# Binding the decay differences in VectorE's order, and taking the first token tile's low inputs last in the mixer's output product

## The chip, the cores and the metric

The kernel runs on one core of one Trainium2 chip. The metric is the device time of one execution in microseconds (us), median over several runs. The engines are named as in the profile: PE is TensorE (PEld its weight loads), DVE is VectorE, ACT is ScalarE, POOL is GpSimd, SP is the engine whose queue issues most DMAs.

## What is computed

A decoder trunk of two layers over 256 tokens of width 1024, all in float32. Each layer is a half-step SwiGLU feed-forward, a token mixer with two branches side by side, and a second feed-forward:

```python
for l in range(DEPTH):
    h = h + 0.5 * swiglu(rms_norm(h, ffn1_norm[l]), ffn1_w_in[l], ffn1_w_out[l])
    u = rms_norm(h, mix_norm[l])
    (z_s, xbc, dt_s, qkv, z_d, b_d, a_d, gate_s, gate_d) = split(u @ w_in[l])
    y_s = mamba2_branch(z_s, xbc, dt_s, ...)     # SSD scan, 32 heads in 4 groups, chunks of 128
    y_d = deltanet_branch(qkv, z_d, b_d, a_d, ...)  # gated delta rule, 8 heads, chunks of 64
    merged = (sigmoid(gate_s) * (y_s @ ssm_w_branch[l])
              + sigmoid(gate_d) * (y_d @ dn_w_branch[l]))
    h = h + merged @ w_out[l]
    h = h + 0.5 * swiglu(rms_norm(h, ffn2_norm[l]), ffn2_w_in[l], ffn2_w_out[l])
return rms_norm(h, final_norm)
```

Inside the SSD scan each group of 8 heads needs a decay matrix per chunk: the exponential of the differences of a cumulative sum, with a causal mask, times the product of C and B.

```python
seg = a_cum[:, :, :, None] - a_cum[:, :, None, :]
decay = where(causal, exp(where(causal, seg, 0.0)), 0.0)
cb = einsum("bclgn,bcsgn->bclsg", Cc, Bc)
y_diag = einsum("bclsg,bclsgh,bcsghp->bclghp", cb, decay, xdt)
```

## The kernel before

Weights come from memory as tiles of 128 x 1024 float32 (`wraw`). Every float32 product is made of three products of rounded parts: each weight tile is split into a high part (`whi`, a copy on ScalarE) and a low part (`wlo`, a subtraction on VectorE), each input in the same way (`mh` and `ml` in the mixer's output product, `bh` and `bl` in the branches), and TensorE adds high x high, high x low and low x high (`mm3`). Five raw tiles and five split pairs are in flight; the splits are made ahead of the products that use them.

The kernel is written with a tile framework. It sorts each engine's instructions into one fixed queue before the run: it walks them in the order of the program with estimates of its own for their durations, and gives an idle engine the earliest instruction of the program that is ready. So an instruction that stands late in the program can be put early into a queue, wherever the estimate sees a hole. `tc.issue_after(ins)` adds an edge without a semaphore: what is traced inside it comes behind `ins` in the queue of the same engine. On the chip each queue is run in its order.

The mixer follows a list of steps, `ORDER`. The end of it is

```python
R x00 R d1 x01 R d3 R R P R g100 g101 D0 S0 x10 T0 D1
x11 g110 g111 S1 x20 T1 o x21 N D2 y S2 D3 x30 x31 T2 g000 g010 g001 S3 g011 T3
```

`R` is a step of DeltaNet's recurrence over chunks (`recur`); its last steps write the sum `vb` on VectorE from the PSUM bank `ob`. `P` (`ssd_pre`) multiplies B and C for the four groups (`cbb` on TensorE, four PSUM banks in rotation with other tiles named by `trb`) and masks them on VectorE (`cbm`, which is `cbt` in the profile). `Dg` (`decay`) makes group g's decay matrix `dc`, 128 x 2048: a broadcast DMA from `rdram` on SP's queue, then the difference to `ac` (VectorE), a minimum with 0 (VectorE), the exponential (ScalarE) and the product with `cbm` (VectorE). `xgi` projects two of a group's channels and convolves them (`ca` on ScalarE and VectorE, then `xsT` on ScalarE). `Sg` and `Tg` are the two halves of the scan of a group: transposes of `xsT` into `xsb` and the scaled inputs `xD`, `xdt`, `xe`; then the products with `dc` into `ydb`. `zgi` and `gsni` are projections that give gates. `o` and `N` are DeltaNet's branch: `dn_T` turns and splits a pair of heads of `vb` (`oT`, `og`, `bh`, `bl`), and `dn_branch` multiplies with the branch weights (`b`). `y` is `ss_T(0)`, the same for the first piece of the SSD output `yz` (`yT`); the SSD branch itself follows the list. Then `merge` adds the two branches into `tg`, turns them (`mT`) and splits them into `mh` and `ml`, one token tile t of 128 tokens after the other, and `close` runs the output product (`o` in the profile, lines 335 to 337 for high x high, high x low, low x high) through `out_chunks`: first the weight tiles 0 and 1 as one group, both halves n of the output columns, for t = 0 and then for t = 1.

Of the kernel before, what the change touches and what calls it, by code (L numbers as in the profile page):

```python
# [11 lines left out]
ALU = mybir.AluOpType  # L12
# [4 lines left out]
P = 128  # L17
D = 1024
S = 256
# [34 lines left out]
def trunk_kernel(ctx, tc, x, wst, wsm, norms, lpar, rpar, cst, out):  # L54
    nc = tc.nc
    V, A, G, PE = nc.vector, nc.scalar, nc.gpsimd, nc.tensor
# [10 lines left out]
    def act(o, i, func=AF.Copy, **kw):  # L67
        return A.activation(out=o, in_=i, func=func, **kw)  # L68

    def tt(o, a, b, op):  # L70
        return V.tensor_tensor(out=o, in0=a, in1=b, op=op)  # L71
# [4 lines left out]
    def ts(o, a, s1, op0, sc2=None, op1=None):  # L76
        if op1 is None:
            return V.tensor_scalar(out=o, in0=a, scalar1=s1, scalar2=None, op0=op0)
        return V.tensor_scalar(out=o, in0=a, scalar1=s1, scalar2=sc2, op0=op0, op1=op1)

    def f(ap):
        return ap.bitcast(F32)
# [66 lines left out]
    state = {"loaded": 0, "prepped": 0, "taken": 0, "last": None, "hold": False, "behind": {}, "late": {}, "first": 0, "turns": {}, "first_chunk": False, "cap": n_forms}  # L149
# [69 lines left out]
    h = cpool.tile([P, 2, D], F32, name="h")  # L219
# [11 lines left out]
    ident = cs[:, 0:P]  # L231
# [102 lines left out]
    def mm3(ps, lh, ll, rh, rl, start, stop):  # L334
        PE.matmul(ps, lh, rh, start=start, stop=False)  # L335
        PE.matmul(ps, lh, rl, start=False, stop=False)  # L336
        return PE.matmul(ps, ll, rh, start=False, stop=stop)  # L337
# [55 lines left out]
                        cut and a == 0 and kt == 1,  # L393
                    )

    def out_chunks(ps, stat, ks, last, group=1, split=False, first=None):

        for g0 in range(0, len(ks), group):
            kk = ks[g0 : g0 + group]
            ws = [(k, take()) for k in kk]  # L400
            for t in range(2):
                order = [(k, n) for n in range(2) for k in range(len(kk))]
                if t == 1 and not split:
                    m = len(kk) - 2 if len(kk) == NSPL else len(kk)
                    order = [(k, n) for k in range(m) for n in range(2)]
                    order += [(k, n) for n in range(2) for k in range(m, len(kk))]
                order = [(k, n, 0, 512) for k, n in order]
                if t == 1 and split:
                    order = [o for o in order if o[1] == 0]
                    order += [(k, 1, c, c + 256) for c in (0, 256) for k in range(len(kk))]  # L410
                state["sums"] = []
                for k, n, c0, c1 in order:
                    k, (wh, wl) = ws[k]
                    sh, sl = stat(k, t)
                    c = slice(n * 512 + c0, n * 512 + c1)
                    begin = k == 0 if first is None else first and t == n == 1
                    bank = ps[t][n][:, c0:c1]
                    if c0:
                        begin, bank = k == kk[0], ps[2][:, 0:256]
                    ins = mm3(bank, sh, sl, wh[:, c], wl[:, c], begin, k == last)  # L420
                    state["sums"].append(ins)

    def residual(po, nw):
        def add(t):
# [11 lines left out]

    def close(po, stat, n_k, nw):

        out_chunks(po, stat, list(range(2)), n_k - 1, group=2)
        out_chunks(po, stat, list(range(2, n_k - NSPL)), n_k - 1)  # L440
        state["hold"] = True
        out_chunks(po, stat, list(range(n_k - NSPL, n_k)), n_k - 1, group=NSPL, split=nw is None)
        return residual(po, nw)
# [149 lines left out]
    def mixer(l, nxt):  # L593
# [13 lines left out]
        yz = {}  # L607
# [37 lines left out]
        ac = small([P, 2, 40], "ac", 1)  # L645
# [380 lines left out]
        late = {}  # L1026
# [11 lines left out]
        def ssd_pre():  # L1038
            BT, CT = late["BC"][:, 0:4], late["BC"][:, 4:8]
            cbt = slots.tile([P, 3 * GS, P], F32, tag="sF", name="cbt")  # L1040
            late["cbx"] = cbx = cbt[:, 2 * GS :]
            late["cbm"] = cbm = cbt[:, : 2 * GS].rearrange("p (g t) l -> p g t l", g=GS)
            for g in range(GS):
                cbb = trb("cbb")
                PE.matmul(cbb[:, 0 : 2 * P], BT[:, g, 0:P], CT[:, g, :], start=True, stop=True)
                PE.matmul(cbb[:, 2 * P : 3 * P], BT[:, g, P : 2 * P], CT[:, g, P : 2 * P], start=True, stop=True)
                tt(
                    cbm[:, g],
                    cbb[:].rearrange("p (t o l) -> p t o l", t=2, o=2)[:, :, 0, :],
                    U[:, None, :].to_broadcast([P, 2, P]),  # L1050
                    ALU.mult,
                )
                act(cbx[:, g], cbb[:, P : 2 * P])
            yield

        xsT = {}
# [2 lines left out]
        def decay(g):  # L1059
            dc = slots.tile([P, 8, 2, P], F32, tag=("sA", "sB")[g % 2], name="dc")  # L1060
            nc.sync.dma_start(
                dc[:].rearrange("p h t l -> p (h t l)"),
                rdram[8 * g : 8 * g + 8].rearrange("a b -> (a b)").partition_broadcast(P),
            )
            tt(
                dc[:], dc[:],
                ac[:, :, 8 * g : 8 * g + 8].rearrange("p t h -> p h t")[:, :, :, None].to_broadcast([P, 8, 2, P]),
                ALU.subtract,
            )
            dv = dc[:].rearrange("p h t l -> p (h t l)")  # L1070
            ts(dv, dv, 0.0, ALU.min)
            act(dv, dv, AF.Exp)
            tt(dc[:], dc[:], late["cbm"][:, g, None].to_broadcast([P, 8, 2, P]), ALU.mult)
            decs[g] = dc

        def xs_unit(g, i):
# [73 lines left out]
        def dn_T(hp):  # L1150
            bank = trb("oT")
            bv = bank[:].rearrange("p (a c i) -> p a c i", a=2, c=4)
            for c in range(4):
                PE.transpose(bv[:, :, c, :], vb[:, c, hp, :], ident)
            og = tmp2("og")
            stt(og[:], bank[:], dnw, late["zdT"][:, 2 * hp : 2 * hp + 2, :].rearrange("p h t -> p (h t)"), ALU.mult, ALU.mult)
            oh = s2.tile([P, 2, S], F32R, tag="s2", name="bh")
            ol = s2.tile([P, 2, S], F32R, tag="s2", name="bl")
            act(oh[:].rearrange("p a t -> p (a t)"), og[:])
            tt(ol[:].rearrange("p a t -> p (a t)"), og[:], f(oh[:]).rearrange("p a t -> p (a t)"), ALU.subtract)  # L1160
            brT[("d", hp)] = (oh, ol)

        def ss_T(j):
            bank = trb("yT")
            g, k0 = j // 2, (j % 2) * 2
            for k in range(2):
                for t in range(2):
                    c0 = (k0 + k) * P
                    PE.transpose(bank[:, k * S + t * P : k * S + (t + 1) * P], yz[g][:, t, c0 : c0 + P], ident)
            oh = s2.tile([P, 2, S], F32R, tag="s2", name="bh")  # L1170
            ol = s2.tile([P, 2, S], F32R, tag="s2", name="bl")
            for k in range(2):
                w = snw[:, 2 * j + k : 2 * j + k + 1]
                act(oh[:, k], bank[:, k * S : (k + 1) * S], scale=w)
                stt(ol[:, k], bank[:, k * S : (k + 1) * S], w, f(oh[:, k]), ALU.mult, ALU.subtract)
            brT[("s", j)] = (oh, ol)

        def branch(kind, n, mk, tail=1):
            ps = [[accb("b"), accb("b")] for _ in range(2)]
            held = {}  # L1180

            def stat(k, t):
                oh, ol = held[k // 2]
                return oh[:, k % 2, t * P : (t + 1) * P], ol[:, k % 2, t * P : (t + 1) * P]

            made = 1
            for j0 in list(range(n - tail)) + [n - tail]:
                js = range(j0, j0 + (tail if j0 == n - tail else 1))
                while made < min(js[-1] + 2, n):
                    mk(made)  # L1190
                    made += 1
                for j in js:
                    held[j] = brT.pop((kind, j))
                out_chunks(ps, stat, [2 * j + i for j in js for i in range(2)], 2 * n - 1, group=2 * len(js))
            return ps

        def dn_branch():
            ps = branch("d", 4, dn_T)
            m = tg[1]
            for t in range(2):  # L1200
                for n in range(2):
                    sl = slice(n * 512, (n + 1) * 512)
                    stt(m[:, t, sl], m[:, t, sl], 1.0, ps[t][n][:], ALU.add, ALU.mult)
# [49 lines left out]
        ps = branch("s", 8, ss_T)  # L1253
# [185 lines left out]
```

## Time and profile before

| | |
|---|---|
| median of 3 runs | 1543.27 us (1543.04 to 1545.02) |
| the profiled execution | 1541.48 us |
| its span, first to last instruction | 1539.7 us |
| busy: PE, DVE, ACT, POOL | 1522.8, 1229.7, 944.8, 81.8 us |
| mean granted TensorE clock | 0.999 |

The profile comes from one execution. A timeline row gives the start from the span's beginning, the duration, the engine, the line of the kernel, the operation, the tiles written and read, the shapes and a count; in brackets the idle time of the engine before it and what ended it. Many elementwise operations go through helpers, so their line is the helper's (68 for ScalarE, 71, 74 and 78 for VectorE) and the tiles' names tell them apart. A matmul's duration holds its way through the array; successive matmuls overlap, so distances between starts tell what one takes in a row of them. Both layers' mixers run the same queues; the first stands at about 190 to 600 us of the span, the second some 760 us later.

### The profile page before, as it was taken

The page shows a single profiled execution, that of the slowest core. Times are in us where ns is not written, and L with a number is a line of the kernel's source. Part 1 is how long each engine was busy: PE and PEld are TensorE (multiplying, and loading weights), DVE is VectorE, ACT ScalarE, POOL GpSimd, SP SyncE. Part 2 cuts the span into 40 slices and gives each one's busy share as a digit, 9 for nine tenths or more (in the row PEclk, how much of TensorE's full clock was granted, in tenths as well). Part 3 has the DMA queues.
Part 4 walks back from the last instruction along what each step waited for, and adds up shares of the span by engine and source line. Part 5 has one row for each costly group of instructions (what it writes and reads, how often), then busy time and mean ns, then how long its engine had stood idle before and what let it go on. Part 6 is the DMA issues. An engine that isn't in the chain of part 4 may idle for free.

```text
span 1539.7 us, 29072 instructions
## 1 busy us (share of the span) xinstructions
PE 1522.8 (99%) x11473; PEld 1384.4 (90%) x11473; DVE 1229.7 (80%) x1859; ACT 944.8 (61%) x1532; POOL 81.8 (5%) x92
## 2 busy tenths in 40 slices
PE   8999999999999999999999999999999999999998
PEld 7999889999888888999899998899998888899997
DVE  6878769967899766789778887689589996677886
ACT  5655667765665645555555566676756666455565
POOL 0000110000000000000100012010000000000010
PEclk9999999999999999999999999999999999999999
DMA  7687775653565556587867687665345555556785
GB/s 277 190 265 231 226 228 167 187 164 111 178 213 171 163 166 196 185 256 211 261 225 225 208 253 229 197 193 180 117 141 202 179 170 186 176 177 195 247 241 156
DMA packets 98831, 305.73 MB, mean 199 GB/s; under 512 B 22837, under 2 KB 23813, under 8 KB 97670
## 3 DMA queue, kind: packets, MB, share of 16 engines
q1 hardware_dynamic: 93796, 290.95, 57.2%
q0 software_dynamic: 4608, 12.58, 5.1%
q8 instruction: 90, 1.47, 0.4%
q14 instruction: 47, 0.39, 0.1%
q10 hardware_dynamic: 290, 0.33, 0.1%
HBM read 297.72 MB, written 1.92 MB: 195 GB/s over the span
## 4 chain that ended last, share of the span: by engine, by line
PE 89%; DVE 4%; ACT 2%; DMA 2%; issue 1%; SPq 1%; POOL 0%; POOLq 0%; ACTq 0%; DVEq 0%
PE fc L346 10%; PE fc L340 9%; PE fc L345 9%; PE t L366 9%; PE o L337 4%; PE o L335 4%; PE o L336 4%; PE f L366 3%; PE b L335 3%; PE b L337 3%; PE b L336 3%; PE p L336 2%; PE p L337 2%; PE p L335 2%; PE xs L345 1%; PE xs L340 1%
## 5 line engine op out<-in xcount | busy, mean ns | idle before, releaser
L71 DVE TENSOR_TENSOR wlo<-wraw,whi 128x1024 fp32r<-128x1024 f32 x488 | 591.8, 1221 | 186.7 <-ACT whi L68 172.2
L68 ACT ACTIVATE whi<-wraw 128x1024 fp32r<-128x1024 f32 x488 | 511.6, 1059 | 271.0 <-PE fc L345 92.5
L346 PE MATMUL fc<-uW,wlo 128*128 128x256 f32 x1280 | 354.9, 277 | 0.0
L340 PE MATMUL fc<-uW,whi 128*128 128x256 f32 x1280 | 354.1, 277 | 0.0
L345 PE MATMUL fc<-uW,whi 128*128 128x256 f32 x1260 | 348.3, 276 | 0.0
L340 PEld LDWEIGHTS fc<-uW,whi 128*128 128x128 f32 x1280 | 240.5, 188 | 0.8
L346 PEld LDWEIGHTS fc<-uW,wlo 128*128 128x128 f32 x1280 | 240.5, 188 | 0.0
L345 PEld LDWEIGHTS fc<-uW,whi 128*128 128x128 f32 x1260 | 236.5, 188 | 0.8
L366 PE MATMUL t<-whi,uW 128*128 128x512 f32 x512 | 165.3, 397 | 0.0
L366 PEld LDWEIGHTS t<-whi,uW 128*128 128x128 f32 x512 | 95.9, 188 | 21.6 <-issue 1.3
L68 ACT ACTIVATE whi<-wsum 128x1024 fp32r<-128x1024 f32 x64 | 68.0, 1062 | 58.8 <-PE fc L345 32.9
L366 PE MATMUL t<-wlo,uW 128*128 128x512 f32 x256 | 100.2, 392 | 0.0
L71 DVE TENSOR_TENSOR wlo<-wsum,whi 128x1024 fp32r<-128x1024 f32 x64 | 78.2, 1221 | 7.9 <-ACT whi L68 5.6
L335 PE MATMUL b<-whi,bh 128*128 128x512 f32 x192 | 76.1, 398 | 0.3
L336 PE MATMUL b<-wlo,bh 128*128 128x512 f32 x192 | 74.9, 390 | 0.0
L337 PE MATMUL b<-whi,bl 128*128 128x512 f32 x192 | 74.2, 393 | 0.0
L340 PE MATMUL xs<-uW,whi 128*128 128x256 f32 x256 | 72.8, 284 | 0.0
L346 PE MATMUL xs<-uW,wlo 128*128 128x256 f32 x256 | 71.4, 279 | 0.0
L345 PE MATMUL xs<-uW,whi 128*128 128x256 f32 x254 | 70.6, 278 | 0.0
L335 PE MATMUL o<-whi,gh 128*128 128x512 f32 (+1 forms) x160 | 62.0, 388 | 0.0
L337 PE MATMUL o<-whi,gl 128*128 128x512 f32 (+1 forms) x160 | 61.8, 386 | 0.0
L336 PE MATMUL o<-wlo,gh 128*128 128x512 f32 (+1 forms) x160 | 61.7, 386 | 0.0
(337 smaller groups left out, 3291.7 us busy)
## 6 DMA issues: line engine op xcount, KB each, us to landing
wraw<-in_wst_dram SPq DMA_DIRECT2D x504, 512.0 KB, 4.9
wsum<-in_wst_dram SPq DMA_DIRECT2D x16, 512.0 KB, 7.3
wsum<-in_wst_dram POOLq DMA_DIRECT2D x16, 512.0 KB, 8.7
dc<-rdram SPq DMA_DIRECT2D x8, 1024.0 KB, 8.5
nw<-in_norms_dram SPq DMA_DIRECT2D x6, 512.0 KB, 5.9
h<-u POOLq DMA_DIRECT2D x12, 256.0 KB, 6.8
gb<-rdram SPq DMA_DIRECT2D x8, 256.0 KB, 5.6
h<-in_x_dram SPq DMA_DIRECT2D x4, 256.0 KB, 3.7
```

What stands on the lines that cost most here:

```text
L68: return A.activation(out=o, in_=i, func=func, **kw)
L71: return V.tensor_tensor(out=o, in0=a, in1=b, op=op)
L335: PE.matmul(ps, lh, rh, start=start, stop=False)
L336: PE.matmul(ps, lh, rl, start=False, stop=False)
L337: return PE.matmul(ps, ll, rh, start=False, stop=stop)
L340: PE.matmul(ps, wh, mh, start=start, stop=False)
L345: PE.matmul(ps, wh, ml, start=False, stop=False)
L346: PE.matmul(ps, wl, mh, start=False, stop=stop)
L366: ins = PE.matmul(ps[t][:], st, mv, start=k0 == 0 and j == 0, stop=k0 == KT - 2 and j == 5)
```

## The change

It has four edges and one reordering.

- `decay`: the difference of each group gets an edge on VectorE. Group 0's comes behind the last masked product of `ssd_pre`; group 1's behind group 0's minimum; group 2's behind the low part of the last pair of heads in `dn_T`; group 3's behind group 2's product with `cbm` (`late["branch"]` is overwritten in the order of the program).
- `ss_T(0)`: its four transposes come behind the last matmul of DeltaNet's branch on TensorE.
- `close`: in the first group of the output product, for the first token tile, the four products with the low input are issued behind the eight with the high input.

```diff
-    def out_chunks(ps, stat, ks, last, group=1, split=False, first=None):
+    def out_chunks(ps, stat, ks, last, group=1, split=False, first=None, defer=False):
...
-                state["sums"] = []
+                state["sums"], lows = [], []
...
+                    if defer and t == 0:
+                        PE.matmul(bank, sh, wh[:, c], start=begin, stop=False)
+                        PE.matmul(bank, sh, wl[:, c], start=False, stop=False)
+                        lows.append((bank, sl, wh[:, c]))
+                        continue
                     ins = mm3(bank, sh, sl, wh[:, c], wl[:, c], begin, k == last)
                     state["sums"].append(ins)
+                for bank, sl, high in lows:
+                    PE.matmul(bank, sl, high, start=False, stop=False)
...
-        out_chunks(po, stat, list(range(2)), n_k - 1, group=2)
+        out_chunks(po, stat, list(range(2)), n_k - 1, group=2, defer=True)
...
 # ssd_pre, in the loop over g
-                tt(
+                ins = tt(
                     cbm[:, g],
...
+                if g == 3:
+                    late["branch"] = ins
...
 # decay
-            tt(
-                dc[:], dc[:],
-                ac[:, :, 8 * g : 8 * g + 8].rearrange("p t h -> p h t")[:, :, :, None].to_broadcast([P, 8, 2, P]),
-                ALU.subtract,
-            )
+            with ExitStack() as behind:
+                behind.enter_context(tc.issue_after((late["diff"] if g == 1 else late["branch"]).ins))
+                tt(
+                    dc[:], dc[:],
+                    ac[:, :, 8 * g : 8 * g + 8].rearrange("p t h -> p h t")[:, :, :, None].to_broadcast([P, 8, 2, P]),
+                    ALU.subtract,
+                )
             dv = dc[:].rearrange("p h t l -> p (h t l)")
-            ts(dv, dv, 0.0, ALU.min)
+            late["diff"] = ts(dv, dv, 0.0, ALU.min)
             act(dv, dv, AF.Exp)
-            tt(dc[:], dc[:], late["cbm"][:, g, None].to_broadcast([P, 8, 2, P]), ALU.mult)
+            late["branch"] = tt(dc[:], dc[:], late["cbm"][:, g, None].to_broadcast([P, 8, 2, P]), ALU.mult)
...
 # dn_T
-            tt(ol[:].rearrange("p a t -> p (a t)"), og[:], f(oh[:]).rearrange("p a t -> p (a t)"), ALU.subtract)
+            ins = tt(ol[:].rearrange("p a t -> p (a t)"), og[:], f(oh[:]).rearrange("p a t -> p (a t)"), ALU.subtract)
             brT[("d", hp)] = (oh, ol)
+            if hp == 3:
+                late["branch"] = ins
...
 # ss_T
-                    PE.transpose(bank[:, k * S + t * P : k * S + (t + 1) * P], yz[g][:, t, c0 : c0 + P], ident)
+                    with ExitStack() as behind:
+                        if j == 0:
+                            behind.enter_context(tc.issue_after(late["sums"].ins))
+                        PE.transpose(bank[:, k * S + t * P : k * S + (t + 1) * P], yz[g][:, t, c0 : c0 + P], ident)
...
 # dn_branch
             ps = branch("d", 4, dn_T)
+            late["sums"] = state["sums"][-1]
```

## The prediction

> **What bounds the kernel now.** I read the page first: its head and the first line of its first part.
>
> ```profile
> span 1539.7 us, 29072 instructions
> PE 1522.8 (99%) x11473; PEld 1384.4 (90%) x11473; DVE 1229.7 (80%) x1859; ACT 944.8 (61%) x1532; POOL 81.8 (5%) x92
> ```
>
> TensorE is busy for all but 1539.7 − 1522.8 = 16.9 us. The change takes no matmul away, so all that it can win lies in TensorE's idle stretches, and all that it can lose are new ones. The second view is the list of waits, TensorE's alone (total, how often, longest).
>
> ```profile
> PE cbb L1045 <- DVE vb L71: 1.9, 2, 1.3
> PE xsb L1101 <- ACT xsT L68: 1.9, 2, 0.9
> PE o L337 <- DVE ml L71: 0.6, 2, 0.3
> ```
>
> Each comes twice, once per layer, and each lies where the change works: 4.4 us of idle. The rest of the list is the kernel's start and the triangular inverse. Then I read the timeline at these places, engine by engine; a stall is counted from start to start, because a busy row of TensorE contains its pipeline. What a 512-wide matmul takes back to back is the distance of two starts, 574.51 to 574.74 in the rows on the output product below: 0.23 us.
>
> **First place: group 0's difference in front of DeltaNet's output.** VectorE in the first layer, then TensorE in both.
>
> ```profile
> 401.94 2.29 DVE L71 TENSOR_TENSOR dc<-dc,ac 128x2048 f32<-128x2048 f32 x1 [0.79 <-DMA dc<-rdram]
> 404.15 0.68 DVE L71 TENSOR_TENSOR vb<-ob,os 128x512 f32<-128x512 f32 x1
> 406.53 0.42 DVE L71 TENSOR_TENSOR cbt<-cbb,cs 128x256 f32<-128x256 f32 x1
> 408.34 1.22 DVE L78 TENSOR_SCALAR dc<-dc 128x2048 f32<-128x2048 f32 x1
> 413.95 2.28 DVE L71 TENSOR_TENSOR dc<-dc,cbt 128x2048 f32<-128x2048 f32 x1
> ...
> 401.81 0.28 PE L995 MATMUL ob<-vn,AT 128*128 128x128 f32 x1
> 403.80 0.48 PE L366 MATMUL t<-whi,uW 128*128 128x512 f32 x1
> 404.88 0.70 PE L1045 MATMUL cbb<-BC 128*128 128x256 f32 x2 [0.60 <-DVE vb L71]
> 421.70 2.08 PE L1115 MATMUL ydb<-xdt,dc 128*64 128x64 f32 x64
> ...
> 1164.50 0.48 PE L366 MATMUL t<-whi,uW 128*128 128x512 f32 x1
> 1166.25 0.70 PE L1045 MATMUL cbb<-BC 128*128 128x256 f32 x2 [1.28 <-DVE vb L71]
> ```
>
> `ob` is finished at 401.81 + 0.28 = 402.09, but VectorE stands first before the difference, whose broadcast has not landed (0.79), and then works on it; `vb`, queued behind, starts at 404.15 instead of about 402.1. The fourth `cbb` needs the PSUM bank that `vb` frees. TensorE loses 404.88 − 403.80 − 0.23 = 0.85 us, and 1166.25 − 1164.50 − 0.23 = 1.52 us in the second layer, together 2.37.
>
> The change binds this subtraction behind the last `cbt` product (406.53). Then `vb` can run from 402.1 to 402.8, over 1 us ahead of 403.80 + 0.23, when TensorE asks for the bank: I take the whole −2.37. What is late next would be the decay itself. With `vb`, four `cbt` and the small reduction in front, the subtraction runs at about 405 to 407.5, still ahead of the minimum's old start at 408.34. The old chain ended at 413.95 + 2.28 = 416.23, and its reader `ydb` starts at 421.70: 5.5 us of cover, which even the whole 2.29 us moved behind the others doesn't use up. Without that cover it would cost what is over 5.5. The broadcast's DMA is issued by SP as before, since the binding is on VectorE alone; nothing new waits on a semaphore. Bounds: −2.37 and, if some other work fills the hole in front of `vb`, 0. Group 1's subtraction is bound behind group 0's minimum, where its data flow already has it: 0.
>
> **Second place: group 2's difference inside a convolution.** TensorE, VectorE and ScalarE in the first layer; the second repeats it.
>
> ```profile
> 441.12 0.82 PE L1101 MATMUL xsb<-cs,xsT 128*128 128x128 f32 x6
> 443.38 0.28 PE L345 MATMUL xs<-uW,whi 128*128 128x256 f32 x1
> 444.59 0.44 PE L1101 MATMUL xsb<-cs,xsT 128*128 128x128 f32 x2 [0.93 <-ACT xsT L68]
> ...
> 439.83 2.28 DVE L71 TENSOR_TENSOR dc<-dc,ac 128x2048 f32<-128x2048 f32 x1
> 442.03 0.47 DVE L74 SCALAR_TENSOR_TENSOR ca<-xs,lp,ca 128x254 f32<-128x254 f32 x1
> 444.12 0.42 ACT L68 ACTIVATE xsT<-ca 128x256 f32<-128x256 f32 x1 [1.26 <-DVE ca L74]
> ```
>
> The stall is 444.59 − 443.38 − 0.11 = 1.10 us per layer (0.11 for a 256-wide matmul, half of the 0.23). The subtraction holds the convolution up by 442.03 − 439.83 = 2.20. Bound behind the last DeltaNet split it leaves that place, and `xsT` could be ready at 444.12 + 0.42 − 2.20 = 442.34, before TensorE's 443.49: then all 1.10 goes. But the order of TensorE's queue is made by a scheduler from its own estimates; if it sees `xsT` earlier, it puts these two transposes straight behind the six, which end at 441.12 + 0.82 = 441.94, and the wait is 442.34 − 441.94 = 0.40, a gain of 0.70. I take −0.75 per layer, near the smaller gain because that queue is the likelier one: −1.5 in all; bounds −2.2 and 0 (the whole lag kept).
>
> **Third place: groups 2 and 3 now come later.** VectorE and ScalarE as they stand, TensorE's reader, then busy time by stage (PE, PEld, DVE, ACT in this order).
>
> ```profile
> 465.81 2.28 DVE L71 TENSOR_TENSOR dc<-dc,cbt 128x2048 f32<-128x2048 f32 x1
> 470.05 2.28 DVE L71 TENSOR_TENSOR dc<-dc,ac 128x2048 f32<-128x2048 f32 x1
> 475.65 0.68 DVE L71 TENSOR_TENSOR bl<-og,bh 128x512 fp32r<-128x512 f32 x1
> 487.62 1.22 DVE L78 TENSOR_SCALAR dc<-dc 128x2048 f32<-128x2048 f32 x1
> 492.93 2.29 DVE L71 TENSOR_TENSOR dc<-dc,cbt 128x2048 f32<-128x2048 f32 x1 [0.68 <-ACT dc L68]
> ...
> 489.68 1.28 ACT L68 ACT_TABLE_LOAD   x1
> 490.97 1.92 ACT L68 ACTIVATE dc<-dc 128x2048 f32<-128x2048 f32 x1
> 493.24 1.99 ACT L68 ACTIVATE whi<-wraw 128x1024 fp32r<-128x1024 f32 x2
> ...
> 493.99 2.08 PE L1115 MATMUL ydb<-xdt,dc 128*64 128x64 f32 x64
> 519.97 2.08 PE L1115 MATMUL ydb<-xdt,dc 128*64 128x64 f32 x64
> ...
> 470.00:482.00 12.00, 12.00 (x55) 9.88 (x54) 11.71 (x12) 7.58 (x8) 0.00 (x0) 1.00 0.55 163
> 482.00:494.00 12.00, 12.00 (x109) 11.87 (x107) 11.26 (x15) 8.38 (x10) 0.00 (x0) 1.00 0.57 208
> ```
>
> The product at 465.81 and the subtraction at 439.83 are group 2's; 470.05, 487.62 and 492.93 are group 3's. After the change group 2 starts behind `bl` (475.65) and group 3 behind group 2's product. VectorE is full there (11.71 and 11.26 of 12 us). But the three operations of group 2 take 2.28 + 1.22 + 2.28 = 5.78, as do those of group 3 that now leave this stretch, and before 475.65 VectorE gets 2.28 (465.81) + 2.28 (470.05) back, besides 439.83's and group 2's minimum. So `bl` itself comes earlier, and group 2, which in program order stands before the next scan's operations, should have its product out between 484 and 490. Deadline: `ydb` at 493.99. Group 3's deadline is 519.97; it needs 5.78 on VectorE and 1.28 + 1.92 on ScalarE, 9.0 us, and has some 30.
>
> Queued behind a late group 2 would be VectorE's weight splits and, on ScalarE, the next `whi`. Hand-overs that end last cost TensorE between 0.3 and 1.3 us of idle in this trace (the three rows of waits). So per layer the cost lies between 0 and 1.3, and beyond that only in the rival case below; a gain is excluded, because `ydb` at 493.99 follows the matmuls without idle today. I take 0.2 per layer, near the lower end for the freed 4.6 us: +0.4.
>
> ScalarE's row 489.68 prices a change of activation table at 1.28 us. The Trainium skill, "ScalarE: Activation LUTs", section "Table sets: the hidden batching unit", advises batching functions by table set and gives about 2.7 us for a load; by its price group 2's chain would be an estimated 1.4 us longer. The row decides here.
>
> **Fourth place: the output product.**
>
> ```profile
> 571.61 0.68 DVE L71 TENSOR_TENSOR ml<-mT,mh 128x512 fp32r<-128x512 f32 x1
> 571.64 0.39 PE L336 MATMUL o<-wlo,mh 128*128 128x512 f32 x1
> 572.34 0.50 PE L337 MATMUL o<-whi,ml 128*128 128x512 f32 x1 [0.31 <-DVE ml L71]
> 573.78 0.60 ACT L68 ACTIVATE mh<-mT 128x512 fp32r<-128x512 f32 x1 [1.52 <-PE mT L1264]
> 574.51 0.39 PE L337 MATMUL o<-whi,ml 128*128 128x512 f32 x1
> 574.74 0.40 PE L335 MATMUL o<-whi,mh 128*128 128x512 f32 x1
> ```
>
> Four high products have run when TensorE meets the first low one; `ml` ends at 571.61 + 0.68 = 572.29, so the stall is 572.34 − 571.64 − 0.23 = 0.47 per layer. With eight high products first, the low ones are due 4 × 0.23 = 0.92 us later than 571.87, and the wait is gone. Next late is the second token tile: its high input ends at 573.78 + 0.60 = 574.38, and its first product (574.74) would now be due at 574.27. So 0.11 comes back: −0.36 per layer, −0.7 in all, bounds −0.94 and 0. The number of matmuls and weight loads stays.
>
> The last edge puts the first four SSD transposes behind DeltaNet's last matmul; all four are issued either way: 0.
>
> **Sum.** −2.37 − 1.5 + 0.4 − 0.7 = −4.2 us against the profiled execution (1541.48 us, 1.8 around its span): 1537.3. The median of the runs shown is 1543.27, 1.8 higher, so I forecast 1543.27 − 4.2 = 1539.1.
>
> **Rivals.** A, slower: group 2's chain is taken up only after the next scan's inputs, in the slot where group 3 has it today, and its exponential falls behind the two `whi` at 493.24, which end at 495.23. Then come 1.28 + 1.92 + 2.28: the product ends at 500.7, and `ydb`, fixed in TensorE's queue, waits 500.7 − 493.99 = 6.7 us per layer. 13.4 against a gain of 2.37 + 1.5 + 0.7 = 4.6 is +8.8: 1552.1. It is slower by over 0.2% (3.1 us, about what a measurement of this kernel can tell from no change) once the product ends (4.6 + 3.1) / 2 = 3.9 us after TensorE's arrival. For it: VectorE is full there, and group 3's minimum waited from 472.3 to 487.62. Against: the freed time, and group 2's rank before that scan. The gap of 6.7 us would be the longest of the trace, whose granted clock stays at 1.00 in the rows by stage. The Trainium skill, "TensorE: Matmul & The Clock Gate", Part 1, has TensorE at half rate after an idle window of about 3.4 us; that would add an estimated 1.7 us per layer, and no run here shows it.
>
> B, no change to speak of: the transposes move forward with `xsT` and keep their 1.1 us, and `ydb` waits 1.3 per layer: 1543.27 − 2.37 − 0.7 + 2.6 = 1542.8. For it: the queue's order and the lag come from the same estimates.
>
> C, the binding doesn't free `vb`, because other ready work fills the hole: −4.2 + 2.37 = −1.8, 1541.5. Against: nothing else ran on VectorE while it stood 0.79.
>
> **How the numbers follow.** Forecast 0.60; B 0.16 and C 0.10, both within 0.2%; A 0.10, and 0.04 for a rearranged queue that costs as much elsewhere. Faster 0.60, within 0.2% 0.26, slower 0.14. The low end has every stall gone at no cost, −2.37 − 2.2 − 0.94 = −5.5, and 0.9 for the spread of the runs (half of the 1.98 between 1543.04 and 1545.02): 1536.9. The high end takes in B, with the same 0.9: 1543.7.
>
> **What would show it.** Right: no wait of `cbb` on `vb` and of `o` on `ml` in TensorE's list, that of `xsb` shorter; group 2's subtraction behind `bl`, its product before `ydb` is due; TensorE idle for about 12.7 us instead of 16.9. Wrong: a wait of `ydb` on `dc`, or of matmuls on `wlo` or `whi`, in these stretches.

## The result, and the profile after

The changed kernel took 1549.51 us (median of 6 runs, 1547.75 to 1550.64) against 1543.45 for the kernel before in the same comparison: a ratio of 1.0037, interval 1.0024 to 1.0050. It is slower by 6.1 us where 4.2 us less were forecast. The profiled execution took 1547.75 us, its span is 1546.0, so against the profile of before it is 6.3 longer. First the head of the page and the line of the engines.

```profile
span 1546.0 us, 29072 instructions
PE 1524.1 (99%) x11473; PEld 1385.8 (90%) x11473; DVE 1230.9 (80%) x1859; ACT 945.0 (61%) x1532; POOL 82.2 (5%) x92
```

TensorE's list of waits (total, how often, longest):

```profile
PE b L335 <- ACT bh L68: 5.2, 2, 2.7
PE t L366 <- DVE ca L74: 2.5, 2, 1.3
PE xsb L1112 <- ACT xsT L68: 1.4, 2, 0.7
```

The work is the same, instruction for instruction. The waits of `cbb` on `vb` (1.9) and of `o` on `ml` (0.6) are gone, that of `xsb` went from 1.9 to 1.4: these gains came. Two new waits, one of each kind per layer, are larger than all of them: the first product of DeltaNet's branch `b` waits for its high copy `bh`, and a gate projection `t` waits for a convolution `ca`. Neither is where the prediction looked for trouble. The timeline of after at three places, TensorE first:

```profile
404.28 0.60 PE L1052 MATMUL cbb<-BC 128*128 128x256 f32 x2
461.30 0.50 PE L335 MATMUL b<-whi,bh 128*128 128x512 f32 x1 [2.50 <-ACT bh L68]
461.64 0.40 PE L336 MATMUL b<-wlo,bh 128*128 128x512 f32 x1
461.87 0.39 PE L335 MATMUL b<-whi,bh 128*128 128x512 f32 x1
...
495.90 1.27 PE L1126 MATMUL ydb<-xdt,dc 128*64 128x64 f32 x36
506.50 0.47 PE L366 MATMUL t<-whi,uW 128*128 128x512 f32 x1 [1.29 <-DVE ca L74]
...
455.73 0.74 DVE L74 SCALAR_TENSOR_TENSOR og<-oT,lp,zdT 128x512 f32<-128x512 f32 x1
457.60 1.22 DVE L71 TENSOR_TENSOR wlo<-wraw,whi 128x1024 fp32r<-128x1024 f32 x1
482.28 2.29 DVE L71 TENSOR_TENSOR dc<-dc,cbt 128x2048 f32<-128x2048 f32 x1 [0.79 <-ACT dc L68]
497.77 2.28 DVE L71 TENSOR_TENSOR dc<-dc,cbt 128x2048 f32<-128x2048 f32 x1
504.28 2.46 DVE L74 SCALAR_TENSOR_TENSOR ca<-xs,lp,ca 128x255 f32<-128x255 f32 x6
...
456.63 2.74 POOL L210 TENSOR_TENSOR srr<-sss,mhalf 128x2 f32<-128x2 f32 x1 [21.25 <-DVE sss L79]
459.40 1.33 ACT L68 ACTIVATE yz<-yz,srr 128x512 f32<-128x512 f32 x2 [1.96 <-POOL srr L210]
460.64 0.61 ACT L68 ACTIVATE bh<-og 128x512 fp32r<-128x512 f32 x1
```

The row at 404.28 has no wait: `cbb` no longer stands behind the difference. `ydb` at 495.90 has none either, because group 2's product (482.28) is done 11 us earlier: the slower rival of the prediction, a late product that `ydb` waits for, did not happen. What happened stands in the last three rows. ScalarE has the scaling of `yz` in front of `bh`; the scaling waits 1.96 us for GpSimd's power `srr`, whose row takes 2.74 us; so `bh` starts at 460.64 and `b` at 461.30, 2.50 us late. The copy's input is not late: `og` is done at 455.73 + 0.74 = 456.47, and ScalarE is idle from 459.40 − 1.96 = 457.44, ahead of 458.80, when TensorE runs dry. In the kernel before the same two steps stand the other way round, with two table loads and group 2's exponential ahead of them:

```profile
450.49 1.28 ACT L68 ACT_TABLE_LOAD   x1
451.78 1.92 ACT L68 ACTIVATE dc<-dc 128x2048 f32<-128x2048 f32 x1
453.71 1.28 ACT L68 ACT_TABLE_LOAD   x1
458.76 0.62 ACT L68 ACTIVATE bh<-og 128x512 fp32r<-128x512 f32 x1
460.30 1.34 ACT L68 ACTIVATE yz<-yz,srr 128x512 f32<-128x512 f32 x2 [0.61 <-POOL srr L210]
458.66 1.61 POOL L210 TENSOR_TENSOR srr<-sss,mhalf 128x2 f32<-128x2 f32 x1 [25.77 <-DVE sss L79]
500.43 2.46 DVE L74 SCALAR_TENSOR_TENSOR ca<-xs,lp,ca 128x255 f32<-128x255 f32 x6
```

With the exponential gone from there, the scaling stands first. The last row is the second cost: the six convolution steps that free TensorE's accumulators ran at 500.43, and in after run at 504.28, behind group 3's product (497.77).

The second layer adds a third cost, the clock. TensorE's rows there:

```profile
1224.37 0.50 PE L335 MATMUL b<-whi,bh 128*128 128x512 f32 x1 [2.70 <-ACT bh L68]
1225.08 0.63 PE L335 MATMUL b<-whi,bh 128*128 128x512 f32 x1
1225.51 0.63 PE L336 MATMUL b<-wlo,bh 128*128 128x512 f32 x1
```

Busy time by stage, two rows of layer 2 and then two of layer 1 (the length, then PE, PEld, DVE, ACT, POOL; the figure behind the five engines' is the granted clock):

```profile
1221.35:1224.76 3.41, 0.71 (x5) 0.43 (x4) 0.94 (x2) 2.29 (x5) 1.08 (x1) 1.00 0.75 227
1224.76:1228.17 3.41, 3.41 (x10) 2.64 (x9) 3.41 (x7) 1.66 (x4) 0.00 (x0) 0.50 0.20 80
456.76:460.17 3.41, 2.04 (x19) 1.80 (x17) 2.05 (x2) 1.45 (x3) 2.60 (x1) 1.00 0.47 119
460.17:463.58 3.41, 2.28 (x10) 1.91 (x11) 2.30 (x5) 3.01 (x5) 0.00 (x0) 1.00 0.63 222
```

From 1225.08 to 1225.51 are 0.43 us, from 461.64 to 461.87 were 0.23. Summed over the nine matmuls that ran so, the low clock cost 1.65 us. Behind the like gap of layer 1 it did not fall; the last section shows why.

Start to start, the sum for the profiled execution is: `b` +2.36 and +2.55 (2.67 and 2.87 less 0.31 before), clock +1.65, `t` +1.45 and +1.42, `cbb` −0.85 and −1.52, `xsb` −0.5, `o` −0.96: together +5.6 of the 6.3. The rest is about the pace of the projections of x30 and x31, about 114 ns a matmul before and 119 after, 0.4 us per layer. What sets that pace is open: the kernel with the output product's reordering alone has the one in its first layer and the other in its second.

### The profile page after: what moved, and what is told of

It reads as the page before. It is cut to its first block, busy times and chain, and to the rows that moved or that the text cites. A ratio compares the mean times of both kernels' runs of the same rounds, so it can differ in the third digit from the quotient of the medians.

```text
span 1546.0 us, 29072 instructions
## 1 busy us (share of the span) xinstructions
PE 1524.1 (99%) x11473; PEld 1385.8 (90%) x11473; DVE 1230.9 (80%) x1859; ACT 945.0 (61%) x1532; POOL 82.2 (5%) x92
## 4 chain that ended last, share of the span: by engine, by line
PE 66%; DVE 8%; ACT 4%; issue 2%; DMA 1%; SPq 1%; POOL 0%; POOLq 0%; ACTq 0%; DVEq 0%
PE fc L346 7%; PE fc L340 7%; PE fc L345 7%; PE t L366 6%; PE o L337 3%; PE o L335 3%; PE o L336 3%; PE b L335 3%; PE b L336 3%; PE b L337 3%; DVE ca L74 2%; PE f L366 2%; DVE wlo L71 2%; PE p L336 1%; PE p L337 1%
```

## The experiments

Two theories. Theory 1: the cost lies in places of the later queues, which the edges rearranged (the scaling in front of `bh`, group 3 in front of the convolutions); put those right and the forecast gain appears. Theory 2: VectorE has no slack from about 408 to 508 us, so any work that is moved behind `vb` or into that stretch comes back as a wait somewhere. Ratios are to the kernel before on the same chip, with a 95% interval.

**After once more**, unchanged.

> The changed kernel once more, nothing altered. Theory 1 (ScalarE's order): in each layer the first product of DeltaNet's branch waits 2.5 to 2.9 us for bh, which stands behind the scaling of yz, which waits for GpSimd's power; where that gap is long enough the granted clock falls for some us, which differs from run to run: 1547.5 to 1551 us. Theory 2 (VectorE is late by the moved groups, and TensorE waits for whatever comes last): the same time, but the waits differ in place from those of the first profile.

1549.55 us, 1.0037 (1.0023 to 1.0051); span 1548.8, with the same waits to 0.2 us. It is 2.8 longer than the first profile, mainly because the clock fell in both layers: 13 matmuls lost 2.60 us behind the gap of layer 1, 8 lost 1.56 behind that of layer 2, 4.2 us against 1.65.

**Edges for groups 0 and 1 only.**

```diff
+                if g in (0, 1):
                     behind.enter_context(tc.issue_after((late["diff"] if g == 1 else late["branch"]).ins))
```

> The differences of groups 2 and 3 are unbound again; groups 0 and 1, the transposes of the SSD branch and the reordered output product stay as in the change. Theory 1: both new waits are gone (b on bh back to 0.3 us, no wait of t on a convolution), the gains of the first and fourth place stay: 1543.4 - 2.4 - 0.9 = about 1540, ratio 0.998. Theory 2: VectorE is as full as before at these places, so also about 1540. Rival (the first group's binding, the transposes or the output product carry the loss): 1546 or more.

1547.36 us, 1.0026 (1.0017 to 1.0035): missed by 7 us. `bh` and `ca` are in order, but there are other waits:

```profile
PE t L366 <- DVE wlo L71: 2.5, 2, 1.8
PE xsb L1113 <- ACT xsT L68: 2.3, 2, 1.2
```

Group 1's minimum now stands behind the scan's operations and its exponential has table loads of its own; group 2's difference now stands in front of group 1's product, and there VectorE waits 1.34 us for its broadcast. The weight splits queue up behind. So the edges of groups 0 and 1, with the output product's reordering and the transposes' edge, end 4.3 us above before (1547.36 against 1543.11) with none of the other two groups' edges in place. That is the rival of the expectation: these parts carry a loss of their own.

**Edges for groups 2 and 3 only**, without the other edits.

```diff
+                if g in (2, 3):
                     behind.enter_context(...)
```

> Only the differences of groups 2 and 3 are bound; all else as before the change. Theory 1 and 2: the whole loss without the gains of the first and fourth place, with that of xsb (2.2): + 4.8 for bh, + 2.9 for t, 0 to 3 for the clock, - 2.2: 1549 to 1552. Rival (another part carries the loss): within 2 us of 1543.4.

1550.47 us, 1.0042 (1.0030 to 1.0054), as expected: `t` on `ca` 3.7 and `b` on `bh` 2.7 in total, and a low clock in both layers. So these two edges alone make the kernel 7.4 us slower (before, 1543.11).

**The copy first**: after, with the scaling of group 1's scan bound behind DeltaNet's first `bh`.

```diff
             rsqrt(rr[:], ss[:], [P, 2])
+            if g == 1:
+                yield                      # resumed behind dn_T(0)
+            with ExitStack() as behind:
+                if g == 1:
+                    behind.enter_context(tc.issue_after(late["first"].ins))
                 for t in range(2):
                     yv = yz[g][:, t, :]
                     act(yv, yv, scale=rr[:, t : t + 1])
...
 # dn_T
+            if hp == 0:
+                late["first"] = first      # the copy into bh
```

> The changed kernel with one thing more: on ScalarE the scaling of yz by group 1's scan is queued behind the first high copy bh of DeltaNet's branch, so ScalarE doesn't reach GpSimd's power first. Theory 1: the wait of b on bh falls from 2.7 to under 0.6 us per layer and the clock stays at 1.00; 4 to 6 us less than the changed kernel, 1543 to 1545.5. Theory 2 (VectorE is late, og and bh with it): the wait stays above 1.5 us, 1547 or more.

1548.94 us, 1.0036 (1.0025 to 1.0046). The wait moved instead of going:

```profile
PE t L366 <- DVE ca L74: 5.1, 4, 2.3
PE b L337 <- DVE bl L71: 1.5, 2, 0.8
PE b L335 <- ACT bh L68: 1.2, 2, 0.7
```

TensorE reached the gate projection 1.3 us earlier (its stall starts at 503.64, not 504.95), and the convolutions stood where they had stood (503.91, in after 504.28). This spoke for theory 2.

**The output product's reordering alone**, all four edges and that of `yT` taken out.

> The kernel before with only the second edit: the output product takes the first token tile's low inputs last; no difference is bound. Both theories: the two waits of o on ml (0.6 us in the profile of before) go and nothing else moves, because the edit is far from the decay products: 0.6 to 0.95 us less than the kernel before of this job, some 1542.4 us. If the edit costs something of its own in the other half of its group, the time is at or above before.

1542.68 us, 0.9992 (0.9983 to 1.0000): 1.0 less, as expected, and at the edge of what can be told. Of the parts that were run by themselves it is the only one that pays.

**The pair first.** Groups 0 and 1 stay behind `cbb`, but as a pair; groups 2 and 3 are as before, the output product as in after; the edge on the transposes is out.

```diff
+            for e in (0, 1) if g == 0 else (g,):   # difference, minimum, exponential
+                ...                                # group 0 behind cbb, group 1 behind that minimum
+            # group 0's product behind group 1's minimum; step D1 is group 1's product alone
```

> The second edit, and groups 0 and 1 bound as one pair: difference, minimum and exponential of group 1 stand ahead of group 0's product, so that the two exponentials share a table load as in the kernel before; groups 2 and 3 and the yT transposes are as in the kernel before. Theory 1 (the costs come from what the edges moved elsewhere: group 1's minimum behind the scan, groups 2 and 3 into a later stretch): the wait of cbb on vb goes (0.9 and 1.5 us), those of o on ml go (0.6 to 0.95), no wait of t on wlo: 1539.5 to 1540.5. Theory 2 (VectorE has no slack after 408 us, so that any work moved behind vb returns as a wait of TensorE further on): the 2.3 us difference taken out of the idle place at 402 returns as a wait on wlo, xsT or bl, and the time is 1542.5 to 1545.

1547.15 us, 1.0021 (1.0013 to 1.0030): neither. The waits on `vb` and `ml` are gone, that on `wlo` does not come, yet `b` on `bh` is there again with 5.2 us although groups 2 and 3 are bound to nothing. VectorE is 1.5 us behind at group 0's minimum (409.88 against 408.34), of which 1.0 is there ahead of any edge (the last products into `ob` start at 401.90, in before at 400.93); group 2's exponential has come to stand behind the scaling (467.62), and scaling and copy are swapped.

**Group 3 later**: after, with the step `D3` behind `x30 x31` in `ORDER`.

> After, with group 3's decay product listed behind the convolutions of x30 and x31 in the order written out by hand. Theory 1 (the convolutions stood behind group 3's three steps in VectorE's queue): the waits of t on ca (1.45 and 1.42 us) go, those of b on bh stay: 1546 to 1547. Theory 2 (VectorE is full from 470 to 508 us, and TensorE waits for whatever comes last): a wait of the same size stands at wlo, at xsb or at group 3's own ydb, and the time stays at 1549 to 1550.

1549.10 us, 1.0037 (1.0022 to 1.0052). The wait on `ca` is gone, as theory 1 said, and the time is that of after, as theory 2 said:

```profile
PE b L335 <- ACT bh L68: 7.8, 4, 2.5
```

Two new waits on `bh` of 1.4 us have come, at 534 us and in the second layer, again behind a scaling of `yz` that waits for its power, and the clock fell in both layers (1.6 to 1.7 us each).

**Both cures**: the copy first and group 3 later.

> After, with group 1's scaling behind DeltaNet's first high copy (as in the run with the copy first) and group 3's decay product behind the convolutions. Theory 1: of the copy-first run's 1548.9 us the waits on ca (2.4 and 0.5 us in each layer) go, those on bh and bl (1.6 us in each layer) stay: 1542.5 to 1544. Theory 2: no gain beyond 1 us, 1547.5 to 1549.

1545.05 us, 1.0009 (1.0000 to 1.0017). One cure alone had given 0.6 or 0.4 us, which is within the intervals, the two together give 4.5. That is 1 us above what theory 1 expected and 2.5 below theory 2. What is left is smaller waits, with no low clock behind them:

```profile
PE t L366 <- DVE wlo L71: 2.1, 2, 1.1
PE b L337 <- DVE bl L71: 1.5, 2, 0.8
PE b L335 <- ACT bh L68: 1.4, 2, 0.7
```

**Half the difference moved**: the pair kernel, with the first four heads of group 0's difference left in front of `vb`.

```diff
+                for h0, h1 in ((0, 4), (4, 8)) if e == 0 else ((0, 8),):
+                    # only the second half is bound behind cbb
```

> The pair-first kernel, but with group 0's difference cut into two halves of four heads: the first half stays in VectorE's idle place ahead of vb, and only the second is bound behind the last product of cbb. Theory 2 (VectorE has no slack from 408 us on; what counts is how much of its work moves behind vb): 1.2 us move instead of 2.3, the wait of cbb on vb (0.9 and 1.5 us) goes nearly whole, the high copy bh keeps its place ahead of the scaling of yz, and the waits on xsT and bh stay near those of before (1.1 and 0.3): 1540 to 1541.5. Theory 1 (the order of the later queues alone decides): the same queue orders as before, so the same 1540 to 1541.5; above 1543 speaks against both.

1545.62 us, 1.0010 (1.0001 to 1.0019): missed, mostly. VectorE in front of `vb`, both layers:

```profile
404.42 1.23 DVE L71 TENSOR_TENSOR dc<-dc,ac 128x1024 f32<-128x1024 f32 x1 [0.88 <-DMA dc<-rdram]
1167.76 1.23 DVE L71 TENSOR_TENSOR dc<-dc,ac 128x1024 f32<-128x1024 f32 x1 [2.19 <-DMA dc<-rdram]
```

By what was expected, a time above 1543 speaks against both theories. In the first layer the shorter difference is enough, and the wait of `cbb` is gone; in the second it stays with 1.2 us, because there `vb` is held up by the landing of the broadcast, for which half an instruction waits as a whole one does. The rest is `xsT`, 1.9 us late in each layer, with a low clock behind the second. Profiled executions differ, too: this one took 1548.13, 2.5 above its median, and was 2.4 us behind before the first layer's scan began.

**Less work for VectorE.** An edit to weigh the theories: the minima taken out, in before and in after; the exponential is scaled by 0.01. Both kernels leave out a part of the computation, so only their times count.

```diff
-            ts(dv, dv, 0.0, ALU.min)
-            act(dv, dv, AF.Exp)
+            act(dv, dv, AF.Exp, scale=0.01)
```

> The kernel before without the minimum of the four decay differences; the exponential is scaled by 0.01 so that it stays finite. It leaves that part of the computation out and is the partner of the next run: VectorE has 4.9 us less to do in each layer. Theory 2: the waits of TensorE that VectorE ends (cbb on vb, xsb on xsT, o on ml: some 4.4 us in all) shrink by half: 1540.5 to 1542.5. Theory 1: the same waits, 1543 to 1544.

> After without the four minima, in the same way. In ScalarE's queue the scaling of yz still stands ahead of DeltaNet's first high copy. Theory 2 (VectorE full): with 4.9 us a layer less on VectorE the waits of t on ca go and those of b on bh fall below 1.5 us, so that after's gains (cbb, ml) show: within 1.5 us of the light kernel before. Theory 1 (the place of the copy behind the scaling is the cost): the waits of b on bh stay at 2.5 us and the granted clock falls behind them: 3 to 5 us above the light kernel before.

Before without minima: 1551.96 us, 1.0049 (1.0036 to 1.0061), 8.1 *more* with 4.9 us less work in each layer. Without the minimum the scheduler puts group 2's exponential and its two table loads at 439.04 to 443.55, in front of the `xsT` that `xsb` asks for: that wait is 2.6 us in layer 1, 4.4 in all, with a low clock behind both, 1.6 us each. After without minima: 1543.41 us, 0.9998 (0.9989 to 1.0007). As a pair they miss their purpose, since the queues differ in more than the minima; theory 1's "3 to 5 above the light kernel before" is wrong by its sign, and so is theory 2's "within 1.5 us". Less work on VectorE doesn't make the time shorter by itself. But the light after is 6.1 us under after: there the waits on `ca` and `xsT` are gone, as theory 2 said, though whether for the lighter work or for the other queues is not shown. The wait on `bh` stays:

```profile
PE b L335 <- ACT bh L68: 4.9, 2, 2.4
```

VectorE, GpSimd and ScalarE ahead of it:

```profile
458.00 0.75 DVE L74 SCALAR_TENSOR_TENSOR og<-oT,lp,zdT 128x512 f32<-128x512 f32 x1
458.17 0.69 POOL L210 TENSOR_TENSOR srr<-sss,mhalf 128x2 f32<-128x2 f32 x1 [23.85 <-DVE sss L79]
458.97 1.32 ACT L68 ACTIVATE yz<-yz,srr 128x512 f32<-128x512 f32 x2
```

Here the power takes 0.69 us and the scaling waits for nothing; TensorE still waits 2.4 us for `bh` behind it. Only half of that is the place in ScalarE's queue: `og` is done at 458.75, where after has 456.47, and in the scaling's place the copy would have started at 458.97 instead of 460.20, 1.2 us earlier. The other half would stay, because `og` comes after TensorE has run dry (at 458.44).

**The pair with the copy first**: the pair kernel plus the binding of the copy-first run, nothing else.

> The pair-first kernel with the scaling of group 1's scan bound behind DeltaNet's first high copy on ScalarE. Theory 1: the waits of b on bh (2.6 us in each layer, and 1.4 us of low clock behind one) go: 1541 to 1542.5. Theory 2: VectorE is still 2.3 us behind, other waits take their place: 1544.5 to 1547.

1541.61 us, 0.9984 (0.9976 to 0.9993): as theory 1 said, 5.5 us under the pair kernel and 2.2 under before. ScalarE of the pair kernel:

```profile
461.25 1.33 ACT L68 ACTIVATE yz<-yz,srr 128x512 f32<-128x512 f32 x2 [0.52 <-POOL srr L210]
462.49 0.61 ACT L68 ACTIVATE bh<-og 128x512 fp32r<-128x512 f32 x1
```

ScalarE of this one:

```profile
459.45 0.62 ACT L68 ACTIVATE bh<-og 128x512 fp32r<-128x512 f32 x1
460.07 1.34 ACT L68 ACTIVATE yz<-yz,srr 128x512 f32<-128x512 f32 x2
```

TensorE's waits in it:

```profile
PE xsb L1122 <- ACT xsT L68: 2.6, 2, 1.3
PE b L335 <- ACT bh L68: 1.5, 2, 0.8
```

The wait on `bh` fell from 5.2 to 1.5, and with it went the low clock (1.6 us in the pair kernel's profile). Theory 2 keeps a part: the wait on `xsT` is 1.9 in before and 2.6 here, which fits VectorE's later start but was not tested by itself, and in after, as the copy-first run shows, the stretch up to 506 us was full enough to take one cure's gain back. The gain of group 0's edge is real, but only where the queue behind it is held.

## Why the prediction was wrong, point by point

*The first place was right in its gain and wrong in its cost.* `cbb` gained 0.85 and 1.52, the −2.37 forecast. The cost was set at 0 because the decay chain had 5.5 us of cover before `ydb`. That cover held, though the subtraction ran later than the forecast's 405 to 407.5, behind a second step of `vb` that waits for GpSimd:

```profile
406.37 0.69 DVE L71 TENSOR_TENSOR vb<-vb,so 128x512 f32<-128x512 f32 x1 [0.79 <-POOL so L210]
406.98 2.28 DVE L71 TENSOR_TENSOR dc<-dc,ac 128x2048 f32<-128x2048 f32 x1
```

But the work that moved also rearranged the queues behind it. The zero was wrong: with the edges of groups 0 and 1 and none for groups 2 and 3 the kernel is 4.3 us above before, and the pair kernel, which has this gain and the output product's, is 3.5 above. With the copy held in its place the pair kernel is 2.2 below.

*The second place* came to −0.25 per layer, not −0.75. The difference left, as said, but group 1's exponential came in with table loads of its own, right where the splits and convolutions for this `xsT` begin, and `xsT` was no earlier than before (444.12). That the one is the reason of the other is argued from the rows:

```profile
428.84 1.28 ACT L68 ACT_TABLE_LOAD   x1
432.08 1.28 ACT L68 ACT_TABLE_LOAD   x1
444.47 0.42 ACT L68 ACTIVATE xsT<-ca 128x256 f32<-128x256 f32 x1 [0.80 <-DVE ca L74]
```

*The third place is the step that failed most.* Its two edges alone make the kernel 7.4 us slower, where +0.4 was taken for them here and −1.5 at the second place. "I take 0.2 per layer" was a cost for TensorE's wait at the end of the moved chain, `ydb`, with its deadline of 493.99. That deadline was kept. The chain's start was left without a price: group 2's exponential and two table loads, 4.5 us of ScalarE at 450.49 to 455, left the queue in front of the copy, and copy and scaling changed places. This goes through all the runs in which nothing binds the copy: where group 2's exponential stands ahead (before, groups 0 and 1 only, the output product alone, half moved, the light before) the copy comes first; where it comes later (after, groups 2 and 3 only, the pair first, group 3 later, the light after) the scaling does. That is a coincidence in ten queues; what in the scheduler's estimates makes it so stays open. Nor was the middle of the chain priced: group 3 has "some 30" us of slack for itself, but the six convolutions behind it have none, because two accumulators hang on them. Each layer pays 2.4 to 2.6 us for the first, 1.4 for the second, and up to 2.6 of low clock. The two cures together take 4.5 of the 6.1 us back; where the other 1.6 lie was not taken apart.

*The fourth place* was right and even a little low: the kernel with that edit alone is 1.0 us faster (0.7 forecast), and start to start 0.47 and 0.49 per layer are gone.

*The last edge*, on the transposes, was put at 0 and has no run of its own. In the kernel with the edges for groups 2 and 3 only, which lacks it, the four `yT` (459.03, 0.63 us) stand in the gap in front of `b`, and TensorE idles there for 1.80 us instead of 2.50. So it may cost some 0.6 us per layer while that gap is there.

*The rivals.* A named the right engine, ScalarE, and the right kind of error, a queue rearranged around a moved exponential, but at the wrong reader; its `ydb` had 11 us to spare. "A rearranged queue that costs as much elsewhere" stood there with a chance of 0.04, without a place: that was the case. The sentence on the clock was used with too long a gap. The Trainium skill ("TensorE: Matmul & The Clock Gate", Part 1) puts the fall to half rate behind an idle window of about 3.4 us and calls the window free-running. That the window runs free agrees with these traces; that it has to be idle for all its length does not: 1.77 us of idle within 3.41 were enough (last section).

## What to carry to other kernels

In a kernel whose queues are made by a list scheduler an ordering edge is two edits: it places one instruction and it frees a hole where that instruction was, and whatever is ready next falls into the hole; price the hole as well as the deadline, by asking who stands behind the moved work on each engine and which banks or copies those steps release. If a gain has been shown at one place and the sum is a loss, bind the step that slipped in front (here one edge, worth 5.5 us) before undoing the gain. And test cures together: the wait that one cure takes away can come back at the next late engine, 0.6 and 0.4 us alone, 4.5 both.

## What was not expected of the hardware

A gap of 2 to 3 us on TensorE can cost more than itself. In the fourteen profiles the granted clock fell to half 13 times inside the mixers, twelve times for 3.41 us and once for 6.83. Some nine 512-wide matmuls then take 0.43 us instead of 0.23, or twice as many 256-wide ones 0.22 instead of 0.11: 1.5 to 1.7 us each time, once 2.6. The length of the gap alone doesn't decide. The clock fell behind eight of ten gaps of 2.4 to 2.7 us (after twice, the pair first, group 3 later, the light after, two layers each), behind gaps of 2.6 and 1.8 in the light before, behind one of two of 1.9 in the half-moved kernel, and with the edges for groups 2 and 3 only behind 1.35 with 0.45 just ahead of it; it did not fall behind the two of 2.25 in the copy-first kernel.

What decides is where the gap lies on a grid. The clock is low once more at the end of every profile, and within each the low stretches start whole multiples of 3.413 us apart (in after 1224.76 and, at the end, 1542.20, 93 steps). If each profile is divided by its grid, TensorE is idle for 1.77 to 2.70 us in the window right in front of each of the 13 falls, and for at most 1.53 in every other window between 150 and 1530 us. The four rows of the section on the result are such windows: layer 2's gap in after lies in one of them (3.41 − 0.71 = 2.70 idle), that of layer 1 is divided between two (1.37 and 1.13). The grid lies differently in each execution, so with a gap of 2.5 us the fall is a matter of luck. Why one low stretch lasted for two windows, with only 0.67 us of idle in the first, is open.

GpSimd's power on 256 numbers takes 0.69 or 0.70 us where VectorE is not in a subtraction of two SBUF tiles as it starts, mostly 1.6 where it starts into one, and 2.74 in after, where two follow each other and the second ends at 457.60 + 1.22 = 458.82, 0.55 before the power's end; behind three in a row (group 3 later, at 512.84) it takes 3.87. A second one does not always go first: with both cures two follow each other at 512.40 and the power takes 1.60. The Trainium skill, "SBUF — State Buffer", section "SBUF: two separate sides", describes this: VectorE with two SBUF inputs and a GpSimd operation that reads SBUF share a pair of ports, and whichever starts first holds it for its whole instruction. The rows agree for GpSimd's side; none shows VectorE held up: in the light before `wlo` starts at 512.43, 0.33 us into a power, and takes its usual 1.23.
